# One scaled token half, and two more pairs as seven products in the second gate-up group

## The chip, the cores and the metric

The kernel runs on one core of one Trainium2 chip. The metric is the device time of one launch in microseconds (us). Smaller is better.

## The reference

One layer of an encoder on `x` of 256 tokens by 2048 features, all in float32: a half-step feed-forward block, a mixer (a gated linear recurrence beside windowed attention), and a second half-step feed-forward block. The change lies in the two feed-forward blocks alone:

```python
def swiglu(x, w_gate_up, w_down):
    gate, up = jnp.split(x @ w_gate_up, 2, axis=-1)
    return (jax.nn.silu(gate) * up) @ w_down

x = x + 0.5 * rms_norm(swiglu(rms_norm(x, pre_norm_ffn1), w_ffn1_gate_up, w_ffn1_down), post_norm_ffn1)
...   # the mixer
x = x + 0.5 * rms_norm(swiglu(rms_norm(x, pre_norm_ffn2), w_ffn2_gate_up, w_ffn2_down), post_norm_ffn2)
```

`w_gate_up` is 2048 x 11264 (gate and up, 5632 columns each), `w_down` is 5632 x 2048.

## The kernel before

**Numbers in two parts.** TensorE (PE) multiplies in a reduced form of float32 (`F32R`). Every operand is therefore split into a high part (ScalarE, ACT, casts: L176) and a low part (VectorE, DVE, subtracts: L177), both in `split_act`. One product of two blocks is three matmuls (high by high, high by low, low by high), in `Blocks.three` (L442).

**Gate-up.** The columns are worked off in groups `g` = 0 to 10 of 512 gate and 512 up columns (`NG` = 11). In a group the 2048 features are eight pairs `u` = 0 to 7 of two 128-row blocks `k`. The output of a group are four banks `c[m][n]`: token half `m` (128 tokens each) by gate or up `n`. A pair is multiplied in one of two ways:

- *plain* (`Blocks.plain`): eight block products, 24 matmuls. Its weights (one `raw` tile of 128 x 2048) are split in two halves of 128 x 1024.
- *as seven products* (`Blocks.products`): the 2 x 2 block scheme with seven products in place of eight, 21 matmuls. It needs sums of blocks on both sides. On the weights: the first block is split alone (`prepare`, a split of 128 x 512), a DMA issued by GpSimd (POOL) adds two weight blocks in place (L953), DVE adds twice (L967, L968), and three halves of 128 x 1024 are split (`splits`). On the tokens: `sums_in(u)` forms the sums of both token halves on DVE (L1069, L396, L399, L400) and splits them (tile `xs`), once per pair and FFN; the result serves all groups.

`MIXED_IN = (2, 4, 5, 6)` are the pairs that are made as seven products. Group 0 makes none so, group 1 makes pairs 2 and 4 so, and groups 2 to 10 all four. `PREPARED` says at what place in the sequence of loads a mixed pair's weights come. Weights rotate through five `raw` tiles; the halves through five buffers each for the high and the low part (`hip`, `lop`): a sixth half is cast only when PE has used the first.

**Scaling.** The norm's factor per token, `rs2` (128 x 2, one column per token half), is known only after group 0 has begun. Group 0 works on unscaled tokens, and its result is scaled by `rs2` in `units`. From group 1 on the tokens carry the power of two of their factor (`two`) and the rest of it (`rest`, between 1 and 2) is applied in `units`. Behind pair 4 of group 0, `power_and_rest` takes `rs2` apart by masks on its bits, `spread(two)` brings the factors along the free axis into `R` (a matmul of ones, L279), and `even(u)` multiplies the token tile of pair `u` (128 x 1024) by `R` in place (L1062), for all eight pairs, each after group 0 has read it. Behind `even` of pairs 2 and 4 comes their `sums_in`.

**The order around the change.** From the first instruction of group 1 the order on every engine is written out by hand (`tc.manual_schedule`): each engine runs its instructions in the order of the code. `first_pairs(g)` makes pairs 0 and 1, `pair_ahead(g, u)` for u = 2 to 5 splits the weights of pair u + 1, then issues the matmuls of pair u, then the last third of the splits of u + 1. In group 1, `sums_in` of pairs 5 and 6 stands behind `pair_ahead` of pairs 4 and 5. Pair 6 follows, then `boundary`, which adds the four product banks into the output banks on DVE (L1167 to L1177) while pair 7 is multiplied bank by bank: the first block waits for L1167, the second for L1170.

Of the kernel before, what the change touches and what calls it, by code (L numbers as in the profile page):

```python
# [11 lines left out]
F32 = mybir.dt.float32  # L12
F32R = mybir.dt.float32r
U8 = mybir.dt.uint8
I32 = mybir.dt.int32
BF16 = mybir.dt.bfloat16
AF = mybir.ActivationFunctionType
ALU = mybir.AluOpType
AX = mybir.AxisListType

P = 128
D = 2048
T = 256
# [14 lines left out]
def hymba_layer_kernel(  # L38
# [25 lines left out]
    nc = tc.nc  # L64
# [11 lines left out]
    def nm(s):  # L76
        uid[0] += 1
        return f"{s}_{uid[0]}"
# [4 lines left out]
    def pb():  # L83
        return psum.tile([P, 512], F32, tag="pb", name=nm("pb"))
# [16 lines left out]
    ones = const.tile([P, P], F32, tag="ones", name="ones")  # L101
# [35 lines left out]
    R = const.tile([P, T], F32, tag="R", name="R")  # L137
    scales = const.tile([P, 8], F32, tag="scales", name="scales")
    rs2, two, rest = (scales[:, 2 * i : 2 * i + 2] for i in range(3))

    def load(src, between=None, pool=rawp, **kw):
        raw = pool.tile([P, 2048], F32, tag="raw", name=nm("raw"), **kw)
        if len(src.shape) == 4:

            dst = raw.rearrange("p (a n b) -> p a n b", a=src.shape[1], n=src.shape[2])
            parts = [(dst[:, a], src[:, a]) for a in range(src.shape[1])]
        else:
            parts = [(raw.rearrange("p (a b) -> p a b", a=src.shape[1]), src)]
        for i, (to, of) in enumerate(parts):
            if i and between:  # L150
                between()
            nc.sync.dma_start(to, of)
        return raw
# [21 lines left out]
    def split_act(hi, lo, src):  # L175
        nc.scalar.copy(hi, src)  # L176
        nc.vector.tensor_tensor(lo, src, hi.bitcast(F32), ALU.subtract)  # L177
# [87 lines left out]
    def power_and_rest():  # L265

        for part, a, b in ((two, 0x7F800000, 0), (rest, 0x007FFFFF, 0x3F800000)):
            nc.vector.tensor_scalar(
                part.bitcast(I32), rs2.bitcast(I32), a, b, ALU.bitwise_and, ALU.bitwise_or
            )  # L270

    def spread(factor=rs2):

        ps = pb()
        for m in range(2):
            nc.vector.tensor_scalar(
                R[:, m * P : (m + 1) * P], ident, factor[:, m : m + 1], None, ALU.mult
            )
        nc.tensor.matmul(ps[:, :T], ones, R, start=True, stop=True)  # L279
        nc.vector.tensor_copy(R, ps[:, :T])  # L280


    def xcol(xt, k, part=None):
# [110 lines left out]
    def sums_of(u, w):  # L394

        nc.vector.tensor_tensor(  # L396
            w[:, S3::2, :], u[:, 0, :].rearrange("p (m t) -> p m t", m=2), u[:, :, P:T], ALU.subtract
        )
        nc.vector.tensor_tensor(w[:, S2, :], w[:, S1, :], u[:, 0, 0:P], ALU.subtract)  # L399
        nc.vector.tensor_tensor(w[:, S4, :], u[:, 1, 0:P], w[:, S2, :], ALU.add)  # L400
        return w
# [481 lines left out]
    NG = DFF // 512  # L883
# [3 lines left out]
    MIXED_IN = (2, 4, 5, 6)  # L887
# [8 lines left out]
    class Gated(Blocks):  # L896
# [19 lines left out]

        def plan(self):

            self.here = {g: MIXED_IN if g > 1 else MIXED_IN[:2] for g in range(1, NG)}
            wanted = []  # L920
            for g in range(1, NG):
                for u in range(KT // 2):
                    before = PREPARED[u] if u in self.here[g] else u
                    wanted.append((g * KT // 2 + before, g, u))
            self.wanted = [at[1:] for at in sorted(wanted)]
            self.raws, self.firsts, self.split_of = {}, {}, {}
            self.lasting = []
            for pool, n in ((rawp, 3), (self.room, 2)):
                for _ in range(n):
                    raw = pool.tile([P, 2048], F32, tag="raw", name=nm("raw"), bufs=n)  # L930
                    if pool is rawp:
                        self.lasting.append(raw)
                    self.load_next(raw)
# [90 lines left out]
    def ffn(gated, w_dn, post_gain, again, gain=None, lead=None, aside=None):  # L1024

        with ExitStack() as st:
# [9 lines left out]
            def room_for(tag):  # L1036
                return work.tile([P, 512], F32, tag=tag, name=nm(tag))
# [20 lines left out]

            def even(u):

                x = gated.tiles[u].rearrange("p k i t -> p (k i) t")
                nc.vector.tensor_tensor(  # L1062
                    x, x.bitcast(F32), R[:, None, :].to_broadcast([P, 4, T]), ALU.mult
                )

            def sums_in(u):
                x = gated.tiles[u].bitcast(F32)
                whole = room_for("z").rearrange("p (k t) -> p k t", k=2)
                nc.vector.tensor_tensor(whole, x[:, :, 0, :], x[:, :, 1, :], ALU.add)  # L1069
                ws = sums_of(whole, room_for("s").rearrange("p (j t) -> p j t", j=4))  # L1070
                apart = u == MIXED_IN[1]
                w = (gated.room if apart else work).tile(
                    [P, 4, 2, P], F32R, tag="sp", name=nm("xs"), bufs=1 if apart else 3
                )
                split_act(w[:, :, 0, :], w[:, :, 1, :], ws)
                gated.sums[u] = w

            def put_away(u):
                away[u] = dram.tile([P, 1024], F32, tag=f"ht{u}", name=nm("away"))
                nc.sync.dma_start(away[u], hts[u].bitcast(F32).rearrange("p k i t -> p (k i t)"))  # L1080
# [61 lines left out]
            for u in range(gated.pos, KT // 2):  # L1142
                gated.work(u + 1)
                if u == 4:
                    power_and_rest()
                    spread(two)
                for done in {4: (0, 1, 2), 5: (3, 4), 6: (5, 6), 7: (7,)}.get(u, ()):
                    even(done)
                    if done in MIXED_IN[:2]:
                        sums_in(done)  # L1150
                if u == 5 and aside:
                    aside()
# [47 lines left out]
            def pair_ahead(g, u):  # L1200

                ahead = gated.splits(g, u + 1)
                next(ahead)
                if u + 1 == MIXED_IN[1]:
                    gated.prepare(g, MIXED_IN[3])
                next(ahead)
                for one in gated.take(g, u):
                    one()
                for _ in ahead:
                    pass  # L1210
                if g == 1 and u in (4, 5):
                    sums_in(MIXED_IN[u - 2])
                if u == 5 and 1 < g <= AWAY // 2 + 1:
                    put_away(2 * g - 4)
                    put_away(2 * g - 3)
# [156 lines left out]
    def two_banks():  # L1372
        return [[pa(), pa()], [pb(), pb()]]

    gated = Gated(w_ffn1_gate_up[0], two_banks())
# [112 lines left out]
    def again_from(src):  # L1488
# [6 lines left out]

    vbanks = [pa(), pa()]
    xt = ffn(
        gated,
        w_ffn1_down[0],
# [10 lines left out]
    with ExitStack() as s2:  # L1510
# [367 lines left out]
        for hp in range(4):  # L1878
            zf = headpair(2048 + hp * 256, "zf")
            if hp == 1:  # L1880
                g = gates(0)
# [18 lines left out]
        g = gates(1)  # L1900
# [13 lines left out]
        gated = Gated(w_ffn2_gate_up[0], two_banks())  # L1914
# [80 lines left out]
```

## Time and profile before

| | |
|---|---|
| median of 3 runs | 1824.78 us (1824.68 to 1824.95) |
| the profiled execution's own time | 1824.81 us |
| its span, first to last instruction | 1823.0 us |
| PE busy | 1809.6 us (99%), 8432 matmuls |
| DVE busy | 1599.9 us (88%) |
| ACT busy | 1131.8 us (62%) |
| POOL busy | 155.6 us (9%) |
| mean granted TensorE clock | 0.998 |

Times in the views count from the first instruction. In a row of the order of time stand the start, the length, the engine, the line, the operation, what it writes and reads, its shape and how many were merged; in brackets the idle time of the engine ahead of it and what ended it. In the rows of groups the last columns are the busy time, the mean length in ns and the idle time ahead. Busy times of PE take in the pipelining of matmuls: two that follow each other overlap, so a spacing is read from starts. The first FFN's group 1 lies at about 57 to 104 us, the second FFN's at about 1168 to 1215 us.

### The profile page before, as it was taken

What the parts mean: (1) busy time and instruction counts of PE and PEld (TensorE: products, weight loads), DVE (VectorE), ACT (ScalarE), POOL (GpSimd) and SP (SyncE); (2) the same over time, 40 slices, a digit from 0 to 9 for tenths busy, and PEclk for the clock granted to TensorE, in tenths of its full rate; (3) what the DMA queues carried; (4) which work ended last, traced back from release to release, by engine and by line L of the source; (5) the groups of instructions that cost most, each with busy time, mean ns of one, the idle gap of its engine ahead of it and who ended that gap; (6) DMA issues with size and microseconds to landing.
All of it is one profiled execution on the core that took longest, in us unless ns stands there. A gap on an engine that the chain in (4) does not pass through costs nothing.

```text
span 1823.0 us, 23428 instructions
## 1 busy us (share of the span) xinstructions
PE 1809.6 (99%) x8432; PEld 1503.0 (82%) x8432; DVE 1599.9 (88%) x2041; ACT 1131.8 (62%) x1498; POOL 155.6 (9%) x149
## 2 busy tenths in 40 slices
PE   9999999999999999999999999999999999999998
PEld 6888888888888888888888888888888888888886
DVE  7999999999989979477687798999999999999987
ACT  7565666666665657476587556556666666566663
POOL 1011111111011100000000000001111111011010
PEclk9999999999999999999999999999999999999999
DMA  8789999998699986555454456789999898699894
GB/s 303 230 232 285 276 283 252 250 266 246 221 339 272 296 263 210 193 186 173 162 173 150 162 209 245 240 238 266 282 274 268 253 250 251 194 347 296 266 315 132
DMA packets 210420, 444.45 MB, mean 244 GB/s; under 512 B 11656, under 2 KB 46560, under 8 KB 209536
## 3 DMA queue, kind: packets, MB, share of 16 engines
q1 hardware_dynamic: 180032, 385.14, 60.7%
q0 software_dynamic: 30272, 57.82, 18.3%
q8 instruction: 66, 1.08, 0.2%
q14 instruction: 50, 0.41, 0.1%
HBM read 430.31 MB, written 12.60 MB: 243 GB/s over the span
## 4 chain that ended last, share of the span: by engine, by line
PE 95%; ACT 2%; DVE 2%; DMA 1%; issue 1%; SPq 0%; POOL 0%; DVEq 0%; ACTq 0%; POOLq 0%
PE pa L442 41%; PE pb L442 36%; PE pa L310 5%; PE pa L315 3%; PE pa L365 2%; PE pa L364 2%; PE pa L363 2%; DVE l L177 1%; DMA raw<-in_w_ffn_gate_up_dram 1%; PE pa L1117 1%; PE pb L1117 1%; ACT h L176 0%; PE pb L1716 0%; PE pb L1690 0%; PE pb L1794 0%
## 5 line engine op out<-in xcount | busy, mean ns | idle before, releaser
L176 ACT CAST h<-raw 128x1024 fp32r<-128x1024 f32 (+1 forms) x861 | 851.4, 1014 | 470.5 <-PE pb L442 149.8
L177 DVE TENSOR_TENSOR l<-raw,h 128x1024 fp32r<-128x1024 f32 (+1 forms) x861 | 983.7, 1172 | 144.1 <-ACT h L176 111.7
L442 PE MATMUL pa<-h,xt 128*128 128x512 f32 x1104 | 387.6, 392 | 0.2 <-DVE xt L232 0.2
L442 PE MATMUL pb<-h,xt 128*128 128x512 f32 x952 | 340.4, 392 | 0.4 <-DVE pb L1170 0.4
L442 PEld LDWEIGHTS pa<-h,xt 128*128 128x128 f32 x1104 | 207.3, 188 | 44.4 <-DVE xt L232 0.6
L442 PE MATMUL pa<-l,xt 128*128 128x512 f32 x552 | 215.4, 390 | 0.3 <-DVE l L177 0.3
L442 PEld LDWEIGHTS pb<-h,xt 128*128 128x128 f32 x952 | 178.6, 188 | 43.7 <-DVE pb L1177 3.9
L442 PE MATMUL pb<-l,xt 128*128 128x512 f32 x476 | 185.4, 390 | 0.0
L442 PE MATMUL pb<-h,ht 128*128 128x512 f32 x464 | 163.2, 389 | 0.0
L442 PE MATMUL pa<-h,ht 128*128 128x512 f32 x464 | 163.1, 389 | 0.0
L953 POOL DMA_DIRECT2D raw<-in_w_ffn_gate_up_dram x76 | 92.1, 1212 | 736.5 <-DVE l L177 654.1
L310 PE MATMUL pa<-xt,h 128*128 128x512 f32 x512 | 124.4, 393 | 0.2 <-ACT h L176 0.2
L442 PEld LDWEIGHTS pa<-l,xt 128*128 128x128 f32 x552 | 103.7, 188 | 21.0 <-DVE l L177 1.0
L310 PEld LDWEIGHTS pa<-xt,h 128*128 128x128 f32 x512 | 93.8, 188 | 18.6 <-ACT h L176 0.6
L442 PE MATMUL pa<-h,xs 128*128 128x512 f32 x304 | 108.8, 389 | 0.0
L442 PE MATMUL pb<-h,xs 128*128 128x512 f32 x304 | 105.9, 389 | 0.0
L442 PEld LDWEIGHTS pb<-l,xt 128*128 128x128 f32 x476 | 89.4, 188 | 17.1
L442 PEld LDWEIGHTS pb<-h,ht 128*128 128x128 f32 x464 | 87.1, 188 | 18.0
L442 PEld LDWEIGHTS pa<-h,ht 128*128 128x128 f32 x464 | 87.1, 188 | 18.0
L442 PE MATMUL pa<-l,ht 128*128 128x512 f32 x232 | 90.3, 389 | 0.0
L442 PE MATMUL pb<-l,ht 128*128 128x512 f32 x232 | 90.3, 389 | 0.0
L1252 POOL DMA_DIRECT2D raw<-in_w_ffn_down_dram x34 | 41.2, 1212 | 377.2 <-DVE la L177 348.7
(288 smaller groups left out, 2547.9 us busy)
## 6 DMA issues: line engine op xcount, KB each, us to landing
raw<-in_w_ffn_gate_up_dram SPq DMA_DIRECT2D x350, 512.0 KB, 5.9
raw<-in_w_ffn_down_dram SPq DMA_DIRECT2D x88, 1024.0 KB, 7.8
raw<-in_w_mix_in_dram SPq DMA_DIRECT2D x52, 1024.0 KB, 4.9
raw<-in_w_ffn_gate_up_dram POOLq DMA_DIRECT2D x76, 512.0 KB, 8.8
raw<-in_w_ffn_down_dram POOLq DMA_DIRECT2D x34, 512.0 KB, 10.2
raw<-in_w_mix_out_dram SPq DMA_DIRECT2D x16, 1024.0 KB, 5.0
ht<-away SPq DMA_DIRECT2D x24, 512.0 KB, 10.8
away<-ht SPq DMA_DIRECT2D x16, 512.0 KB, 7.1
```

Of the source, the lines that this page charges most:

```text
L176: nc.scalar.copy(hi, src)
L177: nc.vector.tensor_tensor(lo, src, hi.bitcast(F32), ALU.subtract)
L310: nc.tensor.matmul(slot[f], weights(hs, kk, f), xcol(xt, k), start=(k == 0), stop=(k == KT - 1))
L315: nc.tensor.matmul(slot[f][:, 0:T], weights(ls, kk, f), xcol(xt, kh * 8 + kk, 0), start=False, stop=False,)
L363: nc.tensor.matmul(dst, xh, h[:, o : o + n], start=(k == 0), stop=False)
L364: nc.tensor.matmul(dst, xh, l[:, o : o + n], start=False, stop=False)
L365: nc.tensor.matmul(dst, xl, h[:, o : o + n], start=False, stop=(k == KT - 1))
L442: nc.tensor.matmul(self.bank(at), lhs, rhs, start=(n == 1), stop=n in (ends, self.of[at]), skip_group_check=n > ends,)
L953: nc.gpsimd.dma_start(raw[:, 0:1024].rearrange("p (k c) -> p k c", k=2), self.source(u, g)[:, :, 1], accum_op=ALU.add,)
L1117: nc.tensor.transpose(bank[:, o : o + P], zs[m][:, k * P : (k + 1) * P], ident)
L1252: nc.gpsimd.dma_start(raws[i][:, 0:1024].rearrange("p (k c) -> p k c", k=2), Pairs.part(w_dn, u, r)[:, :, 512:1024], accum_op=ALU.add,)
```

## The change

In each of the two FFNs:

- Only the lower token half (tokens 128 to 255, the second of the two) is scaled. `power_and_rest` forms, with four more operations on one column, `ratio` = the lower half's power of two divided by the upper half's, puts `rs2` of the upper half into its column of `rest`, and multiplies the lower half's `rest` by the upper half's power of two. `spread(ratio, 1)` works on 128 columns in place of 256, and `even` multiplies 128 x 512 elements in place of 128 x 1024.
- Group 1 makes pairs 2, 4, 5 and 6 as seven products, as groups 2 to 10 do.
- `sums_in` of pair 5 stands behind `pair_ahead(1, 3)` in place of `pair_ahead(1, 4)`; that of pair 6 stays behind `pair_ahead(1, 5)`.

```diff
+    ratio = scales[:, 6:7]
...
     def power_and_rest():
...
-    def spread(factor=rs2):
+        nc.vector.tensor_scalar(
+            ratio.bitcast(I32), two[:, 0:1].bitcast(I32),
+            0x7F800000, 0x7F800000, ALU.bitwise_and, ALU.bitwise_xor,
+        )
+        nc.vector.tensor_scalar(ratio, ratio, two[:, 1:2], 0.5, ALU.mult, ALU.mult)
+        nc.vector.tensor_scalar(rest[:, 1:2], rest[:, 1:2], two[:, 0:1], None, ALU.mult)
+        nc.vector.tensor_copy(rest[:, 0:1], rs2[:, 0:1])
+
+    def spread(factor=rs2, n=2):
 
         ps = pb()
-        for m in range(2):
+        for m in range(n):
             nc.vector.tensor_scalar(
                 R[:, m * P : (m + 1) * P], ident, factor[:, m : m + 1], None, ALU.mult
             )
-        nc.tensor.matmul(ps[:, :T], ones, R, start=True, stop=True)
-        nc.vector.tensor_copy(R, ps[:, :T])
+        nc.tensor.matmul(ps[:, : n * P], ones, R[:, : n * P], start=True, stop=True)
+        nc.vector.tensor_copy(R[:, : n * P], ps[:, : n * P])
...
         def plan(self):
 
-            self.here = {g: MIXED_IN if g > 1 else MIXED_IN[:2] for g in range(1, NG)}
+            self.here = {g: MIXED_IN for g in range(1, NG)}
+            for u in MIXED_IN:
+                self.sums.setdefault(u, None)
...
             def even(u):
 
-                x = gated.tiles[u].rearrange("p k i t -> p (k i) t")
+                x = gated.tiles[u].rearrange("p k i t -> p (k i) t")[:, :, P:T]
                 nc.vector.tensor_tensor(
-                    x, x.bitcast(F32), R[:, None, :].to_broadcast([P, 4, T]), ALU.mult
+                    x, x.bitcast(F32), R[:, None, 0:P].to_broadcast([P, 4, P]), ALU.mult
                 )
...
                 if u == 4:
                     power_and_rest()
-                    spread(two)
+                    spread(ratio, 1)
...
-                if g == 1 and u in (4, 5):
-                    sums_in(MIXED_IN[u - 2])
+                if g == 1 and u in (3, 5):
+                    sums_in(MIXED_IN[(u + 1) // 2])
```

More of the change, by code (lines that the diff above doesn't have):

```diff
@@ L270, in power_and_rest @@
             )
-    def spread(factor=rs2):
+        nc.vector.tensor_scalar(
+            ratio.bitcast(I32),
+            two[:, 0:1].bitcast(I32),
+            0x7F800000,
+            0x7F800000,
+            ALU.bitwise_and,
+            ALU.bitwise_xor,
+        )
[3 more added lines that the diff above has]
+    def spread(factor=rs2, n=2):
         ps = pb()
-        for m in range(2):
+        for m in range(n):
             nc.vector.tensor_scalar(
```

## The prediction

> **What bounds the kernel now.** I read the page's first part, then the order of time on PE and DVE around the second group of each gate-up stage (the only place where the change puts new work), then the chain of waits there, then the stretch after it.
>
> ```profile
> PE 1809.6 (99%) x8432; PEld 1503.0 (82%) x8432; DVE 1599.9 (88%) x2041; ACT 1131.8 (62%) x1498; POOL 155.6 (9%) x149
> ```
>
> PE is the bound over the span, DVE the next. So twelve matmuls fewer look like twelve spacings won. The order of time on PE at the end of group 1 of the first FFN (start, length, engine, line, operation) says that this does not hold there:
>
> ```profile
> 83.53 0.39 PE L442 MATMUL pa<-h,xt 128*128 128x512 f32 x1
> ...
> 88.97 0.39 PE L442 MATMUL pa<-h,xt 128*128 128x512 f32 x1
> ...
> 95.55 0.39 PE L442 MATMUL pa<-h,xt 128*128 128x512 f32 x1
> 96.14 0.50 PE L442 MATMUL pb<-h,xt 128*128 128x512 f32 x1 [0.20 <-DVE pb L1170]
> ```
>
> Pair 5, plain, runs from 83.53 to 88.97: 24 matmuls in 5.44 us, a spacing of 0.227. From 95.55 to 96.14 is 0.59, so PE lost 0.36 waiting for DVE's add of the third output block (L1170, in `boundary`). The chain of waits of that window follows DVE back from there:
>
> ```profile
> 90.39 0.04 DVE l L177
> ...
> 95.39 0.71 DVE pb L1170
> 96.10 0.04 issue
> 96.14 1.67 PE pb L442 x6
> ```
>
> For the last 5.7 us before that boundary the chain lies on DVE, not on PE. Group 1 is already short of DVE time; here is DVE's order of time in it, with idle time and its releaser in brackets:
>
> ```profile
> 69.52 4.62 DVE L177 TENSOR_TENSOR l<-raw,h 128x1024 fp32r<-128x1024 f32 x4
> 74.17 0.69 DVE L967 TENSOR_TENSOR raw<-raw 128x512 f32<-128x512 f32 x1
> 74.90 0.69 DVE L968 TENSOR_TENSOR raw<-raw 128x512 f32<-128x512 f32 x1
> 75.51 3.64 DVE L177 TENSOR_TENSOR l<-raw,h 128x1024 fp32r<-128x1024 f32 x3
> 80.10 1.22 DVE L177 TENSOR_TENSOR l<-raw,h 128x1024 fp32r<-128x1024 f32 x1 [0.95 <-ACT h L176]
> ...
> 89.44 0.69 DVE L177 TENSOR_TENSOR xs<-s,xs 128x512 fp32r<-128x512 f32 x1 [0.69 <-ACT xs L176]
> 90.39 2.96 DVE L177 TENSOR_TENSOR l<-raw,h 128x1024 fp32r<-128x1024 f32 x3 [0.26 <-ACT h L176]
> 93.27 0.69 DVE L1167 TENSOR_TENSOR pa<-pa,z 128x512 f32<-128x512 f32 x1
> ```
>
> The schedule there is written by hand, and DVE runs exactly in the order of the code, so I can walk its queue with these rows.
>
> **Part 1, PE.** In each FFN pairs 5 and 6 of group 1 become 21 matmuls instead of 24: 2 x 2 x 3 x 0.227 = 2.72 us less PE work in all. It counts only as far as PE sets the end of group 1.
>
> **Part 2, DVE in group 1, the term that decides.** I anchor the walk at the first split of pair 4, the fourth of the row at 69.52: it starts at 69.52 + 4.62 - 1.22 = 72.92. From there to the end of L1170 (95.39 + 0.71 = 96.10, by the chain) are 23.18 us. Behind the anchor the change adds: one 128x512 split, the first block of pair 6 (`prepare`, after the two adds of pair 4); and for pairs 5 and 6 each the adds L967 and L968 and a third 128x1024 split. Prices, start to start: a split of 1024 (4.62 - 1.22) / 3 = 1.13; the two adds 75.51 - 74.17 = 1.34; a split of 512 is 93.27 - 90.39 - 2 x 1.13 = 0.62. Sum 0.62 + 2 x (1.34 + 1.13) = 5.56. What it can fill is the idle 0.95 before 80.10, where pair 5's adds will stand. The waits of 0.69 and 0.26 at each `sums_in` stay: DVE waits for ACT's cast of the sums, then for the next cast, in the same order as now. So anchor to L1170 becomes 23.18 + 5.56 - 0.95 = 27.79 us.
>
> **Part 3, where the anchor moves.** Ahead of it the change adds the first block of pair 5 (0.62) and takes away half of each `even`:
>
> ```profile
> L1062 DVE TENSOR_TENSOR xt<-xt,R 128x1024 fp32r<-128x1024 f32 x8 | 9.5, 1220 | 0.1
> L1069 DVE TENSOR_TENSOR z<-xt 128x512 f32<-128x512 f32 x4 | 2.7, 682 | 0.0
> L184 DVE TENSOR_SCALAR v<-tot 128x1 f32<-128x1 f32 x2 | 0.3, 155 | 0.1
> ```
>
> An operation of 512 elements on the same tile takes 0.68 instead of 1.22, so eight save 4.3 us; the four new one-column operations cost about 0.16 each (nearest row L184), net some 3.7 us per FFN. Little of it passes into group 1. The last `even` cannot start before PE has read pair 7 of group 0, and further on the cast that the anchor needs waits for PE to free its buffer:
>
> ```profile
> 56.57 0.39 PE L442 MATMUL pb<-h,xt 128*128 128x512 f32 x1
> 57.99 1.22 DVE L1062 TENSOR_TENSOR xt<-xt,R 128x1024 fp32r<-128x1024 f32 x1
> 70.81 1.06 ACT L176 CAST h<-raw 128x1024 fp32r<-128x1024 f32 x1 [0.45 <-PE pa L442]
> ```
>
> PE ends pair 7 at 56.96, so the `even` at 57.99 can come 1.03 sooner at most and be 0.54 shorter: 1.57 - 0.62 = 0.95 of lead, anchor at 71.97. By the buffer it is not before 70.81 + 1.06 + 0.03 = 71.90. So L1170 ends at 71.97 + 27.79 = 99.76 instead of 96.10: **3.66 us later**. In the second FFN:
>
> ```profile
> 1167.27 0.39 PE L442 MATMUL pb<-h,xt 128*128 128x512 f32 x1
> 1167.93 1.22 DVE L1062 TENSOR_TENSOR xt<-xt,R 128x1024 fp32r<-128x1024 f32 x1
> 1180.03 4.62 DVE L177 TENSOR_TENSOR l<-raw,h 128x1024 fp32r<-128x1024 f32 x4
> 1181.53 1.06 ACT L176 CAST h<-raw 128x1024 fp32r<-128x1024 f32 x1 [0.98 <-PE pa L442]
> 1190.82 1.23 DVE L177 TENSOR_TENSOR l<-raw,h 128x1024 fp32r<-128x1024 f32 x1 [1.15 <-ACT h L176]
> 1206.10 0.70 DVE L1170 TENSOR_TENSOR pb<-pb,z 128x512 f32<-128x512 f32 x1
> ```
>
> Here the last `even` stands 0.27 behind PE's end (1167.66), so the lead is 0.27 + 0.54 - 0.62 = 0.19: anchor 1183.43 - 0.19 = 1183.24 (the buffer would allow 1182.62). Anchor to L1170 is 23.37 + 5.56 - 1.15 = 27.78; it ends at 1211.02 instead of 1206.80: **4.22 us later**. The bounds of this part: both anchors at the buffer's limit gives 3.59 and 3.60; no lead at all (anchors 0.62 later than now) gives 5.23 and 5.03.
>
> **Part 4, what PE does.** With 21 matmuls pair 5 ends at 83.53 + 4.76 = 88.29, and the first two products of pair 6 at 89.65. The third needs the sums of pair 6, now written by `sums_in` directly before: their split ended at 90.13 and will at 90.13 - 0.95 + 5.56 - 0.95 = 93.79. PE waits 4.1 us there (4.7 in the second FFN), then again some tenths at L1167 and L1170. Behind L1170 everything is as now, since now too PE goes on when L1170 ends; so the delay of L1170 is the delay of the program, and the matmuls saved ahead of it are worth nothing. The sums of pair 5, moved one pair forward, are ready by about 81 and needed at 84.9: no wait.
>
> **Part 5, the rest.** The spreading matmul has half its columns:
>
> ```profile
> 38.57 0.39 PE L442 MATMUL pb<-h,xt 128*128 128x512 f32 x1
> ...
> 39.46 0.40 PE L442 MATMUL pa<-l,xt 128*128 128x512 f32 x1
> ```
>
> It takes 0.89 - 2 x 0.227 = 0.44 between these, so half is 0.22 saved per FFN, on PE's path up to the anchor. SP's order of loads changes only in that pair 5 is loaded before pair 3. POOL issues two more accumulating DMAs per FFN:
>
> ```profile
> DMA to landing us min/median/max: 5.4/8.8/11.2
> ```
>
> Pair 6's is asked for at about 75.6 and wanted at about 87, 11.4 us later, so even the longest is covered; pair 5's has 19 us. ACT's four more casts stand in the time in which it waits for DVE.
>
> **Sum.** 3.66 + 4.22 - 2 x 0.22 = 7.4 us on the profiled execution's own 1824.81 (span 1823.0 and 1.8 around it), which lies 0.03 above the median of the runs, so the same on that: 1832.2.
>
> **Rivals.** *The lead passes whole (no change that can be told).* If neither PE's pace nor the buffers held DVE back, its net 3.7 us would bring the anchor forward by 3.1; L1170 would be 5.56 - 0.95 - 3.1 = 1.5 late, with the spreading 2.6 in both: 1827.4. For it: the 4.3 us of `even` are real DVE time, ahead of group 1. Against it: the rows at 57.99 and 70.81.
>
> *Faster.* If PE stays the bound, the time falls by 2.72, the two waits of 0.36 and the spreading's 0.44: 3.9 us, 1820.9. It decides only where DVE ends L1170 by 94.41, when PE would be through the first block of pair 7; my walk is 5.3 us over that. That would need a different order of DVE's work than the code's.
>
> *The clock drops.* The wait of 0.36 us above changes nothing in the spacing behind it. But PE's first products, from rest, are slow:
>
> ```profile
> 1.38 2.31 PE L130 MATMUL pb<-idle 128*128 128x512 bf16 x5 [1.38 <-DVE idle L124]
> ...
> 5.58 0.81 PE L130 MATMUL pb<-idle 128*128 128x512 bf16 x3
> ```
>
> (2.31 - 0.63) / 4 = 0.42 a product at first, (0.81 - 0.38) / 2 = 0.215 from 5.58 on: half rate for the first three to four microseconds. If a wait of 4 us brings that back, 8 of the 21 matmuls from the wait to the one behind L1170 run at 0.42: 6.3 us from 93.79, to 100.1, 0.35 over L1170's end; two such spells give 7.9 us and 1.9. So 0.4 to 1.9 more in each FFN, 1833.0 to 1836.0. The Trainium skill, in "TensorE: Matmul & The Clock Gate", Part 1, says that an idle window of about 3.4 us puts the array's clock back to half and a busy one releases it; by that rule the waits of 4.1 and 4.7 us may trip it, depending on where they lie in the window. The trace agrees at the start alone; no row of this trace shows it behind a wait.
>
> **Numbers.** DVE-bound as walked 0.72; the same with the clock lost 0.12; lead passes whole 0.08; faster 0.08. About 0.2% (3.65 us) is what a measurement of this kernel can tell from no change; 2.6 us is within it. So faster 0.08, same 0.08, slower 0.84. Above, the range goes to the clock's worst case, 1836.0, which also holds the walk without any lead (1824.8 + 10.3 = 1835.1); below, to 1829.5, half way between the walk at the buffer's limit (1831.6) and the rival whose lead passes whole.
>
> **What would show it.** Right: 8420 PE matmuls; in group 1 of each FFN one wait of PE of about 4 us with the split of the sums (L177, xs) as releaser, waits of tenths at L1167 and L1170, DVE with hardly any idle time but for ACT's casts from the first split of pair 4 on; the next group as now. The `even` rows at about 0.68. Wrong: no PE wait over 1 us in group 1 (then PE stayed the bound); DVE's anchor well before 71.9; a releaser that is a DMA; matmuls spaced 0.42 behind the wait (the clock).

## The result, and the profile after

The changed kernel takes **1835.18 us** (median of 6 runs, 1834.36 to 1836.19) against 1824.90 for the kernel before in the same comparison: a ratio of **1.0056 [1.0045, 1.0067]**, 10.3 us slower. The profiled execution took 1835.45 us, its span is 1833.5 us.

In the changed kernel the lines have moved: the products' matmuls are now L454 (L442 before), the cast and the split L177 and L178 (L176, L177), the two adds on the weights L981 and L982 (L967, L968), `even` L1076, the first add of `sums_in` L1083, the adds of `boundary` for the first and the third block L1181 and L1184 (L1167, L1170), the units' transposes L1131 (L1117).

The page, first and fourth part:

```profile
PE 1811.5 (99%) x8420; PEld 1503.4 (82%) x8420; DVE 1603.4 (87%) x2063; ACT 1137.6 (62%) x1506; POOL 160.4 (9%) x153
PE 90%; DVE 4%; ACT 3%; DMA 2%; issue 1%; POOL 0%; SPq 0%; DVEq 0%; ACTq 0%; POOLq 0%
```

Twelve matmuls fewer, as meant, and yet PE is "busy" 1.9 us longer. The fourth part's chain explains a little: PE has 90% of it (95% before), the rest went to DVE, ACT and DMA. Where the time went is read from the transposes of the units (L1117, now L1131), which PE makes once per group at the same place. The order of time on PE, the kernel before and then after, at the transposes in group 1 and in group 2 of each FFN:

```profile
62.25 0.27 PE L1117 MATMUL pa<-ident,z 128*128 128x128 f32 x1
105.93 0.27 PE L1117 MATMUL pa<-ident,z 128*128 128x128 f32 x1
1172.94 0.27 PE L1117 MATMUL pa<-ident,z 128*128 128x128 f32 x1
1216.68 0.27 PE L1117 MATMUL pa<-ident,z 128*128 128x128 f32 x1
```

```profile
62.70 0.27 PE L1131 MATMUL pa<-ident,z 128*128 128x128 f32 x1
112.69 0.27 PE L1131 MATMUL pa<-ident,z 128*128 128x128 f32 x1
1179.52 0.27 PE L1131 MATMUL pa<-ident,z 128*128 128x128 f32 x1
1227.09 0.27 PE L1131 MATMUL pa<-ident,z 128*128 128x128 f32 x1
```

From one to the next, "group 1" below, were 43.68 and 43.74 us, and are 49.99 and 47.57: **6.31 us longer in the first FFN, 3.83 in the second**. What comes ahead of the first transposes is 0.45 later, and the stretch from the end of the first FFN's group 1 to the second FFN's is 0.18 shorter: 10.4 us in all. All groups after them keep their pace.

Inside the first FFN's group 1, PE's order of time after:

```profile
95.74 0.79 PE L454 MATMUL pa<-h,xs 128*128 128x512 f32 x1 [4.47 <-ACT xs L177]
96.33 0.63 PE L454 MATMUL pa<-l,xs 128*128 128x512 f32 x1
96.76 0.63 PE L454 MATMUL pa<-h,xs 128*128 128x512 f32 x1
...
103.16 0.39 PE L454 MATMUL pb<-h,xt 128*128 128x512 f32 x1
```

PE waits 4.47 us for the sums of pair 6 and then runs at half rate for a while: starts 0.43 apart (96.33 to 96.76) where 0.227 is usual. The granted clock is 0.50 from 94.33 to 101.16 and 1.00 behind that. DVE's order of time, the queue that the prediction walked:

```profile
70.92 4.62 DVE L178 TENSOR_TENSOR l<-raw,h 128x1024 fp32r<-128x1024 f32 x4
...
79.78 0.69 DVE L1083 TENSOR_TENSOR z<-xt 128x512 f32<-128x512 f32 x1
...
82.27 0.69 DVE L178 TENSOR_TENSOR xs<-s,xs 128x512 fp32r<-128x512 f32 x1 [0.69 <-ACT xs L177]
83.23 1.23 DVE L178 TENSOR_TENSOR l<-raw,h 128x1024 fp32r<-128x1024 f32 x1 [0.26 <-ACT h L177]
84.49 0.69 DVE L981 TENSOR_TENSOR raw<-raw 128x512 f32<-128x512 f32 x1
...
95.72 0.69 DVE L178 TENSOR_TENSOR xs<-s,xs 128x512 fp32r<-128x512 f32 x1 [0.68 <-ACT xs L177]
...
101.65 0.70 DVE L1184 TENSOR_TENSOR pb<-pb,z 128x512 f32<-128x512 f32 x1
```

From 79.78 on DVE has no idle time there but for ACT's casts around the two `sums_in`, of which each holds DVE's queue for 83.23 - 79.78 = 3.45 us. The anchor, the last of the four splits of the row at 70.92, starts at 74.32; the third block's add ends at 102.35.

The second FFN, DVE's order and PE's:

```profile
1189.19 1.23 DVE L178 TENSOR_TENSOR l<-raw,h 128x1024 fp32r<-128x1024 f32 x1 [0.39 <-ACT h L177]
...
1216.54 0.70 DVE L1184 TENSOR_TENSOR pb<-pb,z 128x512 f32<-128x512 f32 x1
```

```profile
1210.63 0.80 PE L454 MATMUL pa<-h,xs 128*128 128x512 f32 x1 [3.52 <-ACT xs L177]
1211.22 0.63 PE L454 MATMUL pa<-l,xs 128*128 128x512 f32 x1
1211.65 0.63 PE L454 MATMUL pa<-h,xs 128*128 128x512 f32 x1
...
1217.30 0.50 PE L454 MATMUL pb<-h,xt 128*128 128x512 f32 x1
```

The same wait and a shorter spell of half rate (granted clock 0.50 from 1210.5 to 1213.9); here the third block goes on at 1217.30, right behind DVE's add (1217.24).

### The profile page after: what moved, and what is told of

It is laid out like the page before. It is cut to its first block, busy times and chain, and to the rows that moved or that the text cites. A ratio compares the mean times of both kernels' runs of the same rounds, so it can differ in the third digit from the quotient of the medians.

```text
span 1833.5 us, 23448 instructions
## 1 busy us (share of the span) xinstructions
PE 1811.5 (99%) x8420; PEld 1503.4 (82%) x8420; DVE 1603.4 (87%) x2063; ACT 1137.6 (62%) x1506; POOL 160.4 (9%) x153
## 4 chain that ended last, share of the span: by engine, by line
PE 90%; DVE 4%; ACT 3%; DMA 2%; issue 1%; POOL 0%; SPq 0%; DVEq 0%; ACTq 0%; POOLq 0%
PE pa L454 39%; PE pb L454 34%; PE pa L322 5%; PE pa L327 3%; DVE l L178 2%; PE pa L377 2%; PE pa L375 2%; PE pa L376 2%; DMA raw<-in_w_ffn_gate_up_dram 2%; ACT h L177 1%; PE pa L1131 1%; PE pb L1131 1%; PE pb L1730 0%; PE pb L1704 0%; PE pb L1808 0%
## 5 line engine op out<-in xcount | busy, mean ns | idle before, releaser
L177 ACT CAST h<-raw 128x1024 fp32r<-128x1024 f32 (+1 forms) x869 | 857.1, 1012 | 472.2 <-PE pb L454 159.6
L178 DVE TENSOR_TENSOR l<-raw,h 128x1024 fp32r<-128x1024 f32 (+1 forms) x869 | 990.2, 1169 | 147.6 <-ACT h L177 114.3
L454 PE MATMUL pa<-h,xt 128*128 128x512 f32 x1088 | 382.0, 392 | 0.1
L454 PE MATMUL pb<-h,xt 128*128 128x512 f32 x928 | 332.6, 392 | 0.1
L454 PEld LDWEIGHTS pa<-h,xt 128*128 128x128 f32 x1088 | 204.3, 188 | 43.8 <-DVE xt L233 0.6
L454 PE MATMUL pa<-l,xt 128*128 128x512 f32 x544 | 212.3, 390 | 0.2 <-DVE l L178 0.2
L454 PEld LDWEIGHTS pb<-h,xt 128*128 128x128 f32 x928 | 174.4, 188 | 41.8 <-DVE pb L1191 3.5
L454 PE MATMUL pb<-l,xt 128*128 128x512 f32 x464 | 181.0, 390 | 0.0
L454 PE MATMUL pb<-h,ht 128*128 128x512 f32 x464 | 163.3, 389 | 0.0
L454 PE MATMUL pa<-h,ht 128*128 128x512 f32 x464 | 163.2, 389 | 0.0
L967 POOL DMA_DIRECT2D raw<-in_w_ffn_gate_up_dram x80 | 97.0, 1213 | 742.1 <-DVE l L178 678.1
L454 PE MATMUL pa<-h,xs 128*128 128x512 f32 x320 | 116.1, 393 | 8.0 <-ACT xs L177 8.0
L454 PEld LDWEIGHTS pa<-l,xt 128*128 128x128 f32 x544 | 102.2, 188 | 20.7 <-DVE l L178 1.0
L454 PE MATMUL pb<-h,xs 128*128 128x512 f32 x320 | 113.1, 394 | 0.0
L454 PEld LDWEIGHTS pb<-h,ht 128*128 128x128 f32 x464 | 87.1, 188 | 18.1
L454 PEld LDWEIGHTS pa<-h,ht 128*128 128x128 f32 x464 | 87.1, 188 | 18.1
L454 PEld LDWEIGHTS pb<-l,xt 128*128 128x128 f32 x464 | 87.3, 188 | 16.6
L454 PE MATMUL pa<-l,ht 128*128 128x512 f32 x232 | 90.3, 389 | 0.0
L454 PE MATMUL pb<-l,ht 128*128 128x512 f32 x232 | 90.3, 389 | 0.0
L454 PEld LDWEIGHTS pa<-h,xs 128*128 128x128 f32 x320 | 60.6, 189 | 21.7 <-ACT xs L177 8.8
## 6 DMA issues: line engine op xcount, KB each, us to landing
raw<-in_w_ffn_down_dram POOLq DMA_DIRECT2D x34, 512.0 KB, 10.4
```

Of the source, the lines that this page charges most:

```text
L454: nc.tensor.matmul(self.bank(at), lhs, rhs, start=(n == 1), stop=n in (ends, self.of[at]), skip_group_check=n > ends,)
L967: nc.gpsimd.dma_start(raw[:, 0:1024].rearrange("p (k c) -> p k c", k=2), self.source(u, g)[:, :, 1], accum_op=ALU.add,)
```

## The experiments

The theory: DVE's queue in group 1 sets the time; the matmuls saved count for nothing until DVE has room, and PE's clock for little. Rivals: the scaling itself costs the time; the long wait of PE costs it through the clock. The table gives all runs; group 1 is the distance between the transposes as above, "start" the first transposes of the first FFN. These three columns are read from the one profiled execution of each kernel, the time is the median of its runs.

| kernel | time, us | against before | start | group 1, FFN 1 | FFN 2 |
|---|---|---|---|---|---|
| before | 1824.8 to 1825.0 | | 62.25 | 43.68 | 43.74 |
| after | 1835.18 | 1.0056 [1.0045, 1.0067] | 62.70 | 49.99 | 47.57 |
| E1 scaling alone | 1824.66 | 0.9998 [0.9989, 1.0008] | 62.30 | 43.71 | 43.72 |
| E2 products alone | 1836.44 | 1.0064 [1.0047, 1.0080] | 62.37 | 49.03 | 49.21 |
| E4 sums one pair earlier | 1834.24 | 1.0051 [1.0036, 1.0066] | 62.53 | 48.57 | 47.56 |
| E5 PE kept busy | 1835.11 | 1.0053 [1.0038, 1.0068] | 62.20 | 50.35 | 47.58 |
| E8 one sum left out | 1827.92 | 1.0015 [1.0006, 1.0024] | 62.12 | 46.51 | 44.14 |
| E6 both sums left out | 1822.56 | 0.9987 [0.9977, 0.9996] | 62.23 | 41.95 | 41.80 |
| E3 sums in group 0 | 1830.26 | 1.0029 [1.0018, 1.0040] | 64.52 | 44.84 | 44.60 |
| E7 sums on GpSimd | 1831.47 | 1.0035 [1.0022, 1.0048] | 64.27 | 49.17 | 44.70 |
| E11 sums in group 0, own rooms | 1821.78 | 0.9983 [0.9974, 0.9992] | 62.41 | 42.54 | 41.81 |
| E12 the same, R sooner | 1821.75 | 0.9982 [0.9973, 0.9991] | 63.06 | 42.15 | 41.81 |

**E1 and E2: the two parts apart.** E1 is the changed kernel with the mixing of before:

```diff
-            self.here = {g: MIXED_IN for g in range(1, NG)}
-            for u in MIXED_IN:
-                self.sums.setdefault(u, None)
+            self.here = {g: MIXED_IN if g > 1 else MIXED_IN[:2] for g in range(1, NG)}
...
-                if g == 1 and u in (3, 5):
-                    sums_in(MIXED_IN[(u + 1) // 2])
+                if g == 1 and u in (4, 5):
+                    sums_in(MIXED_IN[u - 2])
```

> Only the scaling part of the change (lower half alone, ratio, halved even); group 1 keeps two pairs as seven products. Theory A (DVE's queue in group 1 sets the end there): group 1 is as before, so the time is near before's. The spreading matmul costs the wait for its factors seen in the changed kernel (0.64 us in the first FFN) less 0.2 in each FFN for half the columns, and the waits of 0.36 at the third output block may go: 1824.0 to 1825.4. Rival (the new scaling, by its own operations or by shifting the loads, makes up the 2.5 us that the first FFN lost more than the second): 1827 or more.

E2 is the kernel before with the same lines the other way round: both token halves scaled, four pairs as seven products, the sums placed as in the changed kernel.

> Only the four pairs as seven products in group 1 and the moved sums; scaling of both halves as before. Theory A: DVE's added work is the same 5.56 us, the halved even bought little, so the add of the third block is 5.2 and 5.0 us late by the bound without lead, and some 0.5 for the clock: 1834.5 to 1836.5, as the changed kernel. Rival (the halved even pays 3.7 us of DVE time in each FFN and hides that much in the changed kernel): 1841 or more.

The scaling alone is worth nothing that can be measured (0.9998), though it takes DVE work out of each FFN's group 0. The products alone cost 5.35 and 5.47 us of group 1. With the scaling added that becomes 6.31 and 3.83: the halved `even` gives 1.6 us back in the second FFN and takes 1.0 in the first. What it takes is seen in the chain of waits ahead of the anchor. First E2, then the changed kernel (start, length, what):

```profile
54.31 4.09 DMA raw<-in_w_ffn_gate_up_dram
...
58.42 0.03 ACT h L176
```

```profile
51.48 8.71 DMA raw<-in_w_ffn_gate_up_dram
...
60.21 0.63 ACT h L177
```

The load that ACT's cast for pair 4 waits for is asked for 2.8 us sooner, as less `even` work suggests, and lands 1.8 us later: 8.71 us instead of 4.09. POOL's order of time shows what it now meets (the accumulating DMA of pair 2, E2 and then after):

```profile
55.65 1.27 POOL L955 DMA_DIRECT2D raw<-in_w_ffn_gate_up_dram  x1 [7.50 <-ACT xs L176]
```

```profile
51.64 1.27 POOL L967 DMA_DIRECT2D raw<-in_w_ffn_gate_up_dram  x1 [3.37 <-DVE s L412]
```

The accumulating DMA too goes out 4 us sooner, 0.16 us behind the load instead of 1.34. What that does is seen in the DMA queues of the changed kernel (packets, MB, share of the 16 engines), first from 52 to 54 us, then from 57 to 60:

```profile
q1 hardware_dynamic: 378, 0.74, 103.4%
```

```profile
q0 software_dynamic: 184, 0.38, 68.2%
q1 hardware_dynamic: 204, 0.40, 40.6%
```

The loads go through q1, the accumulating DMAs of POOL through q0. Alone, the loads moved 0.37 MB per us, beside the accumulating DMA 0.13. In E2 the load had no such company: q1 moved 0.75 MB from 56.5 to 58.4, q0 nothing. The load also follows the one for pair 0 by 0.77 us in place of 3.77 (issues at 50.71 and 51.48, in E2 at 50.54 and 54.31), so part of its 8.71 us may be waiting behind that one. No run takes the two apart.

In E1, whose group 1 has no new DVE work at all, this cast came at 60.14 and the anchor at 73.65, both later than in the kernel before (57.97 and 72.92). It cost E1 nothing: the idle 0.95 us that DVE has at 80.10 in the kernel before took it up (0.34 is left in E1). The change has filled that idle time with work. In the changed kernel, E4, E5, E6 and E8 the anchor stands 14.10 or 14.11 us behind this cast (74.32 and 60.21 in the changed kernel), whenever the cast comes; so in the first FFN it is the landing of this load that places the anchor. The cast does not come at the same time in each execution, though the code is the same up to there: 60.21, and in E4, E6 and E8 59.09, 59.05 and 60.08. E4's group 1 took 48.57 us in the first FFN, less than E2's 49.03. So the 1.0 us that the halved `even` takes there is that of one execution, and its sign is not settled.

**E4 and E5: the long wait and the clock.** E4 forms the sums of pair 6 one pair earlier:

```diff
-                if g == 1 and u in (3, 5):
-                    sums_in(MIXED_IN[(u + 1) // 2])
+                if g == 1 and u in (3, 4):
+                    sums_in(MIXED_IN[u - 1])
```

> The changed kernel with the sums of pair 6 formed behind pair 4 in place of behind pair 5; no work added or left out. Theory A: DVE has the same work ahead of the third-block add, so that add ends within 0.4 us of where it ends now; the one long wait of PE becomes several shorter ones. If the slow matmuls behind the wait (0.43 us apart for 3 to 5 us) come from the length of a single wait, they go, and the first FFN gains 0.5 to 0.8: 1834.3 to 1835.2. Rival (the loss is that the sums come right before their use): the wait goes with the distance, and the time falls by 4 us or more, 1831 or less.

PE's order of time in E4, first FFN:

```profile
90.56 0.50 PE L454 MATMUL pa<-h,xt 128*128 128x512 f32 x1 [1.11 <-ACT h L177]
91.82 0.50 PE L454 MATMUL pa<-l,xt 128*128 128x512 f32 x1 [0.76 <-DVE l L178]
...
94.41 0.80 PE L454 MATMUL pa<-l,xs 128*128 128x512 f32 x1 [1.62 <-DVE l L178]
95.00 0.63 PE L454 MATMUL pa<-h,xs 128*128 128x512 f32 x1
95.43 0.63 PE L454 MATMUL pb<-h,xs 128*128 128x512 f32 x1
```

One wait has become three of 1.1, 0.8 and 1.6 us, together 3.5, and the half rate is there all the same (granted clock 0.50 from 94.39 to 97.80). The time hardly moves (1834.24 against 1835.18, intervals that overlap; just under theory A's range): the same DVE work, elsewhere in the queue. From the anchor (73.19) to the end of the third block's add (101.23) it takes 28.04 us, in the changed kernel 28.03; group 1 is shorter by what the anchor came sooner. In the second FFN the waits (1.6 us the longest) left the clock at 1.00, and group 1 took 47.56 us, in the changed kernel with its half rate 47.57.

E5 gives PE seven products of zeros to do ahead of the wait, added into a bank where they change nothing (R's unused half is set to zero for it):

```diff
             for i in order:
                 at, left, right = seven[i]
+                if i == 3 and u == 6 and getattr(self, "g", 0) == 1:
+                    for _ in range(FILL):
+                        nc.tensor.matmul(self.bank(("p", 0))[:, 0:P], R[:, P:T], ident, ...)
                 self.three(at, *left, *right)
```

> The changed kernel with seven products of zeros (float32, 128 columns, added to the first product bank, so nothing changes in the result) ahead of the third product of pair 6 in group 1, where PE waits 4.5 and 3.5 us. Theory A with the clock as a second term: PE is not at rest any more, the matmuls behind the wait are 0.227 apart instead of 0.43, the third block starts right behind the third-block add (now 0.77 behind it in the first FFN), and that add ends where it ends now: 1834.2 to 1834.9 and less spread between runs. Rival (the slow matmuls have another cause than PE's rest, such as their operands): 0.43 apart as now, 1835 to 1836.

PE's order of time in E5, first FFN, then second:

```profile
96.09 0.50 PE L458 MATMUL pa<-h,xs 128*128 128x512 f32 x1 [2.93 <-ACT xs L177]
...
102.76 0.50 PE L458 MATMUL pb<-h,xt 128*128 128x512 f32 x1 [0.47 <-DVE pb L1194]
```

```profile
1210.48 0.66 PE L458 MATMUL pa<-h,xs 128*128 128x512 f32 x1 [1.96 <-ACT xs L177]
1210.93 0.63 PE L458 MATMUL pa<-l,xs 128*128 128x512 f32 x1
1211.36 0.64 PE L458 MATMUL pa<-h,xs 128*128 128x512 f32 x1
```

In the first FFN the half rate is gone, and PE simply waits for DVE's add (L1194) instead. In the second FFN starts stayed 0.43 apart behind the wait, and group 1 took 47.58 as without the filling. 1835.11 us is the time of the changed kernel and lies outside theory A's range. In the profiled execution the anchor came 0.36 us later than in the changed kernel (74.68), and so did the end of the third block's add (102.71 instead of 102.35). From there to the next transposes are 9.84 us in E5 (to 112.55), 9.83 in the kernel before (96.10 to 105.93) and 10.34 in the changed kernel (to 112.69). So the half rate cost 0.5 us in the first FFN, and nothing in the second (9.85 there, 9.88 before): a small part of the 10.3.

**E6 and E8: less DVE work in group 1.** The sums of pairs 5 and 6, or of 6 alone, are not formed; existing ones are read in their place.

```diff
-                if g == 1 and u in (3, 5):
-                    sums_in(MIXED_IN[(u + 1) // 2])
+                if g == 1 and u == 3:                      # E6
+                    gated.sums[5], gated.sums[6] = gated.sums[2], gated.sums[4]
...
+                if g == 1 and u == 3:                      # E8
+                    sums_in(5)
+                    gated.sums[6] = gated.sums[5]
```

> The changed kernel without the sums of pairs 5 and 6: group 1 and all later ones read those of pairs 2 and 4 in their place, so the output is not the layer's; all matmuls, splits, adds and DMAs of the change stay. It prices what the change would give if DVE had room. Theory A: 2 x 3.43 us leave DVE's queue in group 1, the third-block add comes at about 95.5 minus what PE still holds it back, PE waits under 1 us in group 1: 1821.3 to 1823.5, below before. Rival (loads or buffers hold group 1 back): 1826 or more.

> The changed kernel without the sums of pair 6 alone (those of pair 5 are read in their place, so the output is not the layer's). Theory A: one dose of 3.43 us less in DVE's queue in each FFN moves the third-block add by 3.4 us, and the clock's 0.5 goes with the long wait: 1827.3 to 1828.7. Rival (only the place of these sums right before their use costs): the whole loss goes, 1823 or less.

DVE's third-block add, in the changed kernel at 101.65, in E8 and in E6:

```profile
98.08 0.70 DVE L1184 TENSOR_TENSOR pb<-pb,z 128x512 f32<-128x512 f32 x1
```

```profile
93.62 0.70 DVE L1184 TENSOR_TENSOR pb<-pb,z 128x512 f32<-128x512 f32 x1
```

The add comes forward by 3.57 us with the first `sums_in` taken away and by 4.46 with the second. Of that the anchor itself moved by 0.13 and 1.04 (74.32, 74.19, 73.15), which leaves 3.44 and 3.42 us for a `sums_in`: the 3.45 that it holds the queue (2.5 of work, 0.95 of waiting for ACT's casts). The time follows: 10.3 us slower with two, 2.9 with one, 2.5 faster with none. In E6 the second FFN's group 1 takes 41.80 us, the pace of all later groups (147.74 to 189.55 in the kernel before is 41.81): PE is the bound again, and the twelve matmuls are worth their price. With E2, E4 and E5, which take 28.03 or 28.04 us from the anchor to that add as the changed kernel does, this settles the theory.

**E3 and E7: the sums elsewhere, two misses.** E3 forms them in group 0, as those of pairs 2 and 4:

```diff
-                    if done in MIXED_IN[:2]:
+                    if done in MIXED_IN:
                         sums_in(done)
...
-                if g == 1 and u in (3, 5):
-                    sums_in(MIXED_IN[(u + 1) // 2])
```

> The changed kernel with the sums of pairs 5 and 6 formed in group 0, behind their even, not in group 1. Theory A: 2 x 3.43 us of DVE's queue leave group 1, whose third-block add then comes near 95 in the first FFN, about where PE needs it; group 0 has DVE idle time of about 4.6 us (1.79, 0.73, 1.42, 0.69 in the changed kernel) for 4.9 us of sums. No wait of PE over 1.5 us, clock kept: 1821.5 to 1824. Rival (the loss comes from the third splits and adds, or from the loads of the two pairs, not from the place of the sums): PE still waits several us in group 1, 1830 or more.

1830.26 us, half of the loss. The number lies in the rival's range, but not for the rival's reason: group 1 is only 1.2 and 0.9 us longer than before, and none of PE's waits in it is over 1.2 us. The order of time at the end of group 0, of ACT, DVE and PE:

```profile
59.53 3.04 ACT L177 CAST h<-raw 128x512 fp32r<-128x512 f32 x4 [2.85 <-DMA raw<-in_w_ffn_gate_up_dram]
62.47 0.61 ACT L177 CAST xs<-s 128x512 fp32r<-128x512 f32 x1
```

```profile
63.12 0.69 DVE L178 TENSOR_TENSOR xs<-s,xs 128x512 fp32r<-128x512 f32 x1 [3.67 <-ACT xs L177]
```

```profile
64.52 0.33 PE L1131 MATMUL pa<-ident,z 128*128 128x128 f32 x1 [2.14 <-DVE z L1111]
66.03 0.48 PE L1131 MATMUL pa<-ident,s 128*128 128x128 f32 x1 [1.18 <-DVE s L1111]
```

The sums use the rooms `z` and `s`, which the units need next, so the units cannot begin before pair 6's sums are split; and the cast for these (62.47) came after casts that wait for pair 4's load (59.53). PE waits 2.1 and 1.2 us for the units, the first of them ahead of group 1 as it is counted here.

E7 gives the adds of these sums to GpSimd (and those of the first unit's sums); DVE only splits them:

```diff
+                if g == 1 and u == 2:
+                    aside_sums.append(sums_raw(5, nc.gpsimd))
...
+                if g == 1 and u == 3:
+                    sums_split(5, aside_sums.pop())
+                    aside_sums.append(sums_raw(6, nc.gpsimd))
+                if g == 1 and u == 4:
+                    sums_split(6, aside_sums.pop())
```

> The changed kernel with DVE relieved and nothing left out: the adds of the sums of pairs 5 and 6, and of the first unit's sums in group 1, are made by GpSimd (a 128x512 add of GpSimd took 1.27 us in the trace of before), ahead of their use; DVE only splits them (0.62 each), behind pairs 3 and 4. Theory A: 2 x 2.81 and 1.0 us leave DVE's queue in group 1, the third-block add ends near 95, 1 us sooner than before: 1821.8 to 1824. Rival (GpSimd's adds slow DVE or come late, or hold the accumulating DMAs): 1826 or more.

In the second FFN that worked for the most part (group 1 44.70), in the first it did not (49.17). The execution profiled here (1833.16) is the slowest of five, and 1.6 us behind the changed kernel already at its first transposes (64.27). POOL's order of time in E7, then DVE's:

```profile
68.19 1.23 POOL L408 TENSOR_TENSOR sums<-z 128x256 f32<-128x256 f32 x1
```

```profile
68.32 1.65 DVE L981 TENSOR_TENSOR raw<-raw 128x512 f32<-128x512 f32 x1
...
73.37 6.51 DVE L178 TENSOR_TENSOR l<-raw,h 128x1024 fp32r<-128x1024 f32 x4
```

An add of 0.69 us takes 1.65 beside GpSimd's, and four splits of 4.62 take 6.51. The Trainium skill, "SBUF — State Buffer", section "SBUF: two separate sides", says that a VectorE operation with two inputs from SBUF and a GpSimd operation that reads SBUF exclude each other for a whole instruction. The trace agrees: DVE's add ends at 69.97, 0.55 us after GpSimd's (69.42), as though it had only then begun. The slowing takes half of the gain: from the anchor to the third block's add DVE needs 25.2 us in both FFNs (28.0 in the changed kernel), 2.8 less where the adds given away (2 x 2.81) would make 5.6. The two FFNs differ ahead of the anchor: it stands 9.67 us behind the first transposes in the second FFN, as in the changed kernel, and 14.13 in the first (11.62), with slowed adds and splits of DVE ahead of it.

**E11 and E12: the sums in group 0, with rooms of their own.** From E3 and E6 follows what a version must do: form the sums ahead of group 1, in rooms that nobody waits for, and leave out of group 0 the one step that hangs on ACT's late cast. E11 moves the sums as E3 does, takes the spare rooms from the tile for the units' sums, which is empty then, and splits pair 6's sums in group 1 behind pair 3:

```diff
             def sums_in(u):
...
+                if u in MIXED_IN[2:]:
+                    spare = spare_rooms()
+                    o = 4 + 2 * (u - MIXED_IN[2])
+                    whole = spare[:, o].rearrange("p (k i) t -> p k (i t)", k=2)
+                    room = spare[:, o + 1]
...
+                if g == 1 and u == 3:
+                    sums_split(MIXED_IN[3], later.pop())
```

> As the changed kernel, but the sums of pairs 5 and 6 are formed in group 0, in two spare rooms apiece that no unit uses, and only the last step of pair 6's (one cast and one 0.69 us subtraction) stays in group 1, behind pair 3. Theory (VectorE has no room in group 1, and group 0 lost time in the earlier run with early sums only through shared rooms and one cast late in ScalarE's order): without any sums formed there group 1 came 1.74 and 1.95 us shorter than before; one subtraction in it gives back some 0.7, so about -1.0 and -1.2; group 0 keeps the +0.5 of the wait for R in the first FFN and may gain up to 0.5 more: 1823.0 to 1825.0, at best just under the kernel before. Rival (group 0 has no more room for 4 us of VectorE work, whatever rooms it uses): group 0 of the first FFN ends over 1.5 us later with waits of the transposes for the units' products, 1826 to 1829.

E12 also puts the two one-column operations that only the units' scale needs behind `spread`.

> As the run before it, and the two one-column operations that only the units' scale needs come behind the spreading of the quotient, so that R's matmul is ready sooner. Theory: TensorE's 0.5 us wait for R in group 0 of the first FFN falls by the two operations (0.2 to 0.3 us): 0.2 to 0.4 us under the run before it, which is within what a measurement can tell. Rival (that wait is covered by a later one in the same group): no difference, within 0.2 us.

**1821.78 us, 0.9983 [0.9974, 0.9992]**: 3.0 us faster than the kernel before and 13.4 faster than the change. DVE's order of time and PE's in E11, first FFN (L1201 is here the add for the third block):

```profile
94.39 0.70 DVE L1201 TENSOR_TENSOR pb<-pb,z 128x512 f32<-128x512 f32 x1
```

```profile
95.14 0.50 PE L454 MATMUL pb<-h,xt 128*128 128x512 f32 x1 [0.39 <-DVE pb L1201]
```

The third block begins right behind DVE's add, as in the kernel before, but a microsecond earlier (95.14 instead of 96.14); no wait for `xs`, no half rate. The second FFN's group 1 takes 41.81, all that there is to have. The time is 1.2 us under the expected range: group 1 gained 1.1 and 1.9 us, not 1.0 and 1.2, and group 0 lost 0.16 instead of 0.5. E12 has no wait for R and gained nothing (1821.75): its rival held. E1, E4, E5, E6 and E8 have no such wait either, without this edit, so that it went is not shown to be the edit's doing.

## Why the prediction was right or wrong

*The bound and its sign: right.* DVE sets the end of group 1; E6 and E8 show it by taking its work away.

*Part 1, the saved matmuls: right.* 8420 matmuls, worth nothing in the change. Where DVE has room, group 1 is 1.7 and 1.9 us shorter than before (E6), 1.1 and 1.9 (E11). Of that 1.36 us are the matmuls; the wait of 0.36 for the third block is gone in E6, and E11 still has one in its first FFN.

*Part 2, anchor to the third block's add: right.* 27.79 was walked; measured are 102.35 - 74.32 = 28.03 in the first FFN, and 1217.24 - 1189.19 = 28.05 in the second (27.78 walked). The walk priced each split of 1024 at 1.13 us, start to start; one that an add follows takes 1.26 (83.23 to 84.49), and the change has two more of these.

*Part 3, the anchor: the step that failed, in the first FFN.* It was to start 0.95 us sooner, at 71.97, and started at 74.32, so 2.35 late. The prediction costed `even` as DVE work ahead of the anchor and asked of PE and of the buffers whether the lead could pass; it did not ask what the earlier loads would meet, and part 5 asked that only of the accumulating DMAs and took them as covered. The load for pair 4 took 8.71 us, and the anchor followed its landing. The bound "no lead" (5.23, anchor at 73.54) did not hold it either. E2, where `even` is whole, has its anchor at 73.51; with `even` halved the six traces with the sums in group 1 or left out (the change, E1 with the 0.62 of pair 5's block added, E4, E5, E6, E8) have it between 0.39 us sooner (73.15, E6) and 1.14 later (74.68, E5) than that bound. So the halved `even` has no steady price in the first FFN. In the second FFN the anchor stands at 1189.19, of which 6.58 is what the program had lost by then: 1182.61. That is the buffer's limit (1182.62), 0.6 better than the forecast; so the third-block add came 3.86 later instead of 4.22.

*Part 4, PE's wait: right in kind.* 4.47 and 3.52 us against 4.1 and 4.7, at the product named; it ends with ACT's cast, not with DVE's split, since the first matmul needs the high part alone. Of the waits at the two adds of `boundary` one showed, some 0.25 us at the third block in the second FFN (its product starts 0.48 behind the one at 1216.82); the half rate filled the others, for in the second FFN of E4, at full clock, PE waited 1.28 and 0.46 us there. A wait of 0.68 us for DVE's split in pair 5 of the first FFN (87.10) was not foreseen; it lies ahead of the long wait and adds nothing to it.

*Part 5, the spreading: not to be seen.* The four one-column operations stand ahead of R on DVE, and PE waited for it:

```profile
39.34 0.49 PE L291 MATMUL pb<-R,ones 128*128 128x128 f32 x2 [0.64 <-DVE R L288]
```

The first transposes came 0.45 later, not 0.22 sooner. But E1, E4, E5, E6 and E8, with the same scaling, have no such wait, and their first transposes came at 62.12 to 62.53, around the 62.25 of before; E12 without that wait had them at 63.06, and E7, late from early on, at 64.27. It is a matter of the run; the 0.22 is not to be seen.

*The sum.* 3.66 + 4.22 - 0.44 = 7.4 was forecast; 6.31 + 3.83 + 0.45 - 0.18 = 10.4 came. Of the first FFN's excess of 2.65 (6.31 - 3.66), 2.35 is the anchor and 0.24 the walk; half rate adds 0.5 at the transposes, and the group's late start (0.45) is counted in the start instead. That the time, 3.0 us above the forecast, still lies in the range, 0.8 us under its end, is in part luck: the range reached so far for the clock, which cost 0.5 us in all, and for the walk without any lead (1835.1), which the first FFN overshot (6.25 against 5.23 for the third block's add) and the second undershot (3.86 against 5.03).

*The rivals.* "The clock drops" came true as an event, at 0.43 a product and a granted clock of 0.50 behind waits of 4.47 and 3.52 us. Its price was at the lower end or below: the third block began 0.81 behind DVE's add in the first FFN (0.04 before) and 0.06 in the second, and 0.5 us and nothing of that were left at the next transposes (E5). "The lead passes whole" fell, in the first FFN by a load, and not by PE's pace or the buffers as was argued. "Faster" fell as argued: PE was not the bound until E6 and E11 made it so.

## What to carry to other kernels

Work taken off the engine that is short pays only in the stretch where it is short: the eight halved `even` of group 0 were by themselves worth nothing (E1), four `sums_in` of 3.45 us in the two group 1 decided 12.6 us (1835.18 to 1822.56). Before matmuls are traded for additions, walk the adding engine's queue to the wait that ends the stretch; if it is full, form what is needed a stage earlier, in buffers that nobody there waits for. And where an edit makes a step finish sooner, look at which transfers it triggers sooner, and at what they then run beside.

## What the runs showed of the hardware

- A GpSimd addition holds up VectorE: 0.69 us became 1.65, four splits of 4.62 became 6.51 (E7). Work moved to an idle GpSimd is not free for VectorE.
- PE's half rate needs no single long pause. In E4 three waits of 1.1, 0.8 and 1.6 us with a few matmuls between them brought it too. In E5 a wait of 2.93 us behind seven products did not, while in the second FFN a wait of 1.96 us did. The granted clock was 0.50 for 3.41 us each time, and for twice that in the first FFN of the changed kernel. In the 3.41 us ahead of it PE was busy for 0.34 and 0.03 us (changed kernel), 1.05 (E4) and 1.45 (E5): a stretch that is mostly idle is enough. The Trainium skill, "TensorE: Matmul & The Clock Gate", Part 1, speaks of one idle window of about 3.4 us and of windows that run freely; the second agrees with such differences between the two FFNs, the first is too narrow for E4 and E5, whose windows were not idle throughout.
- A load of 512 KB asked for 2.8 us sooner landed 1.8 us later. Beside an accumulating DMA of POOL the loads moved 0.13 MB per us, alone 0.37 (changed kernel, 57 to 60 us and 52 to 54).
